# A first weight chunk of 768 columns instead of 512 in a two-layer transformer kernel

## The chip, the cores and the metric

The kernel runs on one NeuronCore of a Trainium2 chip. The metric is the device time of one execution in microseconds. A run here is one program that computes both layers from the inputs in HBM to the output in HBM.

## The reference, cut to what matters

The reference has two blocks over a sequence of 256 tokens of width 2048, everything in float32. Only the first block is touched:

```python
proj = x @ w_in + b_in                    # (256, 2048) @ (2048, 5376)
c_val, c_glu, c_gate, q, k, v, a_gate = split(proj, (1024, 1024, 1024, 1024, 128, 128, 1024))
h = c_val * sigmoid(c_glu)
h = causal depthwise convolution of h, 31 taps, per channel, + conv_b
y_conv = silu(layer_norm(h)) * silu(c_gate)
y_attn = sliding_window_attention(q, k, v, sinks) * silu(a_gate)
y = concat([y_conv, y_attn]) @ w_out + b_out
x1 = layer_norm(2 ** 0.25 * x + y)
```

The second block (sparse attention, a gated per-layer embedding, stick-breaking attention) follows from `x1` and is the same in both kernels.

## The kernel before, in words

**Numbers.** Every matmul operand is split into a high and a low part (`fp32r`), and three products are summed: high times high, high times low, low times high. For each weight tile ScalarE makes the high part (line 281) and VectorE the low part (line 282). For the activations the same is done on lines 404 and 405.

**Chunks and granules.** The weight matrices are read in one long list of column chunks, in the order of the dictionaries `CHUNKS_1`, `CHUNKS_O1` and so on. A chunk runs over 16 row tiles (`kt`) of 128 rows. It is cut into granules, each of which is one DMA, one cast (line 281) and one subtraction (line 282). `_group` says how many row tiles go into a granule: 1 for the first chunk `gv0`, 4 for a chunk of 256 columns, 2 for one of 512. So `gv0` has 16 granules of 128x512, and each chunk of 256 columns of `w_in` has 4 granules of 128x1024. `granules` loads up to 3 granules ahead of the one in use and converts up to 2 ahead, fewer at the very start. There are six buffers for raw weights and four each for the high and low parts.

**The first chunk.** `gv0` holds the first 256 columns of the gate of the convolution branch (two column tiles of 128) and the first 256 columns of its values (two more). `gemm_T` keeps the results transposed: for each row tile and each column tile, one matmul with 512 moving columns (line 359: high and low part of x side by side) and one with 256 (line 361). The activations x come in during this chunk: `load_x` fetches row tiles 0, 1, then 2 and 3 together, then pairs, all on the same queue (SP) between the weights. The next chunks are `g1`, `v1`, `g2`, `v2`, `g3`, `v3` (gates and values of the other three quarters, 256 columns each), then `kv`, the queries and gates of the attention (eight chunks) and the gate `cg` of the convolution branch (four chunks).

**PSUM.** `gemm_T` puts the first two column tiles of a chunk into one tile of two banks from the pool `acc` (two such tiles), and each further column tile into a single bank of the pool `aux` (four banks). `total` adds the two halves of a result and the bias, with a branch for a tile of two banks (lines 374 to 381) and one for a list of single banks (lines 370 and 371).

**Side work.** Work for ScalarE and VectorE that isn't a weight conversion is written as generators in lanes of `Side`. At the end of every granule, after its matmuls have been put into the program, `side.pump()` takes a step in every lane, as many `next` calls as the rate of the generator at the head says. What it puts into the program is ordered behind the subtraction of that granule (`issue_after(pace.ins)`).

```python
    def _step(self, q):
        done = 0
        while q and done < q[0][1]:
            try:
                next(q[0][0]); done += 1
            except StopIteration:
                q.popleft()
```

The lane `conv` holds eight generators `conv(ct)`, one for each 128 channels, with 31 taps each (lines 537 and 539) and a rate of 3. `glu(c)` adds two of them as soon as quarter `c` of h is there. After the `cg` chunks `conv_norm()` is added to the same lane with a rate of 1. It has seven steps: (1) sum over the channels, lines 728, 714, 715; (2) the mean, a matmul with a matrix of ones on line 720, copied on 722; (3) subtract the mean, line 735, and square, line 736; (4) sum the squares, line 738, 714, 715; (5) the variance, line 720 again; (6) `rsqrt` (lines 444 to 449), the scaling (line 746), and SiLU (line 750), the product with the gate (line 753) and the split into parts (lines 404 and 405) for channel tiles 0 to 3; (7) the same for channel tiles 4 to 7. What (6) and (7) write is `cact`, row tiles 0 to 7 of the output projection.

**The output projection.** `w_out` is used in two rounds: chunks `a0` to `a3` over row tiles 8 to 15 (the attention's half, four granules each, so 16 granules), and then chunks `c0` to `c3` over row tiles 0 to 7, which need `cact`. Between them stands `side.drain()`, which takes all the steps that are left in any lane, without a pump:

```python
    side.drain("heads")
    for c in range(NB):
        ps = gemm("w_out", f"a{c}", y1)
        ...
    side.drain()
    ln = Norm(0, z, t["ln_g"], t["ln_b"], 0)
    for c, (s, n) in enumerate(SPANS):
        ps = gemm("w_out", f"c{c}", y1)
```

The functions that the change touches:

Of the kernel before, what the change touches and what calls it, by code (L numbers as in the profile page):

```python
# [23 lines left out]
KT = D // P  # L24
# [18 lines left out]
def _c(start, n):  # L43
    return ((start, n),)
# [3 lines left out]
CV, CG, CT, QQ, KK, VV, AG = 0, 1024, 2048, 3072, 4096, 4224, 4352  # L48
# [7 lines left out]
def _twos(name, start):  # L56
# [2 lines left out]


CHUNKS_1 = {
    "gv0": ((CG, 256), (CV, 256)),
    **{f"{n}{c}": _c(o + 256 * c, 256) for c in range(1, 4) for n, o in (("g", CG), ("v", CV))},
    "kv": _c(KK, 256),
    **{f"q0{h}": _pairs(QQ, i) for i, h in enumerate("xy")},
    **{f"ag0{h}": _pairs(AG, i) for i, h in enumerate("xy")},
# [5 lines left out]
CHUNKS_1 = {key: (ranges, ALL) for key, ranges in CHUNKS_1.items()}  # L72
# [52 lines left out]
def _cols(ranges):  # L125
    return sum(n for _, n in ranges)


def _group(ranges, kts):

    if ranges == CHUNKS_1["gv0"][0]:
        return 1
    return min(len(kts), 4 if _cols(ranges) <= 256 else 2)


def _column_tiles(chunks):

    out, at = {}, 0
    for key, (ranges, _) in chunks.items():
        out[key] = at  # L140
        at += _cols(ranges) // P
    return out
# [42 lines left out]
def tile_net(ctx: ExitStack, tc: tile.TileContext, t: dict, out: bass.AP):  # L185
# [17 lines left out]
    def uid(s):  # L203
        count[0] += 1
        return f"{s}_{count[0]}"
# [5 lines left out]
    def short(shape=(P, 384), dt=F32):  # L211

        return half.tile(list(shape), dt, tag="h", name=uid("h"))

    def bank(name, n=512):
        return aux.tile([P, n], F32, tag="aux", name=uid(name))
# [17 lines left out]
    def keep(ap, base, cm, step, op, fill):  # L234
# [13 lines left out]
        for stream, key in _plan()  # L248
        for kts in (STREAMS[stream][key],)
        for g in range(0, len(kts[1]), _group(*kts))  # L250
    ]
    at = [0]
# [42 lines left out]
    def granules(stream, key, events):  # L295

        ranges, kts = STREAMS[stream][key]
        n = _cols(ranges)
        kpg = _group(ranges, kts)
        for g in range(0, len(kts), kpg):  # L300
            if events and g in events:
                events[g]()
            here = at[0]
            assert plan[here] == (stream, key, g)
            for p in plan[here:here + 1 + min(here, AHEAD)]:
                if p not in held:
                    held[p] = fetch(p)
            for p in plan[here:here + 1 + min(here, LOAD)]:
                if p not in held and p not in loaded:
                    loaded[p] = load(*p)  # L310
            hi, lo, pace = held.pop((stream, key, g))
            at[0] += 1
            for j in range(kpg):
                ws = slice(j * n, (j + 1) * n)
                yield kts[g + j], g + j == 0, g + j == len(kts) - 1, hi[:, ws], lo[:, ws]
            with tc.issue_after(pace.ins):
                side.pump()

    def gemm(stream, key, act, events=None, final=False):

        n = _cols(STREAMS[stream][key][0])
        if final:
            ps = [bank("acc") for _ in range(2)]
        else:
            both = acc.tile([P, 2, 512], F32, tag="acc", name=uid("acc"))
            ps = [both[:, tt, :] for tt in range(2)]

        def product(tt, kt, first, last, wh, wl):
            ah, al = act(kt, slice(tt * P, (tt + 1) * P))
            o = ps[tt][:, :n]  # L330
            nc.tensor.matmul(o, ah, wh, start=first, stop=False)  # L331
            nc.tensor.matmul(o, ah, wl, start=False, stop=False)  # L332
            nc.tensor.matmul(o, al, wh, start=False, stop=last)  # L333

        ends = STREAMS[stream][key][1][-_group(*STREAMS[stream][key]):]
        late = []
        for step in granules(stream, key, events):
            late.append(step)
            if step[0] in ends and not step[2]:
                continue  # L340
            for tt in range(2):
                for one in late:
                    product(tt, *one)
            late = []
        return [p[:, :n] for p in ps]

    def gemm_T(stream, key, act, events=None):

        nf = _cols(STREAMS[stream][key][0]) // P
        two = acc.tile([P, 2, 2, S], F32, tag="acc", name=uid("acc"))
        ps = [two[:, f] for f in range(2)]
        ps += [bank("acc").rearrange("p (h s) -> p h s", h=2) for _ in range(2, nf)]
        for kt, first, last, wh, wl in granules(stream, key, events):
            pair, ah = act.both(kt), act(kt, slice(0, S))[0]
            for f in range(nf):
                nc.tensor.matmul(ps[f], wh[:, f * P:(f + 1) * P], pair, start=first, stop=False)  # L359
            for f in range(nf):  # L360
                nc.tensor.matmul(ps[f][:, 0, :], wl[:, f * P:(f + 1) * P], ah, start=False, stop=last)  # L361
        return [two, ps[2:]][:nf // 2]

    def total(out_, ps, bias=None, scale=1.0):

        t = short((P, 2, S))
        out_ = t if out_ is None else out_
        if isinstance(ps, list):
            for f, p in enumerate(ps):
                nc.scalar.activation(t[:, f, :], p[:, 1, :], AF.Identity, bias=bias1[:, bias + f:bias + f + 1])  # L370
                nc.vector.tensor_tensor(out_[:, f, :], p[:, 0, :], t[:, f, :], ALU.add)
            return out_
        if bias is None:
            nc.scalar.activation(t, ps[:, :, 1, :], AF.Copy, scale=scale)  # L374
        else:
            for f in range(2):
                nc.scalar.activation(t[:, f, :], ps[:, f, 1, :], AF.Identity, bias=bias1[:, bias + f:bias + f + 1])  # L377
        if scale == 1.0:
            nc.vector.tensor_tensor(out_, ps[:, :, 0, :], t, ALU.add)  # L379
        else:  # L380
            nc.vector.scalar_tensor_tensor(out_, ps[:, :, 0, :], scale, t, ALU.mult, ALU.add)
        return out_
# [117 lines left out]
    xact = Act()  # L500

    def load_x(kt, n):
        raw = short((P, n, S))
        nc.sync.dma_start(raw, t["xT"][:, kt:kt + n, :])
        xact.put(kt, n, raw)
# [5 lines left out]
    tiles1 = _column_tiles(CHUNKS_1)  # L511
# [20 lines left out]
    def conv(ct):  # L532
        h, o = hT[ct // 4][:, ct % 4, :], cacc[ct // 4][:, ct % 4, :]
        for d in range(TAPS):
            w = convw[:, ct, TAPS - 1 - d:TAPS - d]
            if d == 0:
                nc.vector.tensor_scalar(o, h, w, convp[:, 0, ct:ct + 1], ALU.mult, ALU.add)
            else:
                nc.vector.scalar_tensor_tensor(o[:, d:], h[:, :S - d], w, o[:, d:], ALU.mult, ALU.add)  # L539
            yield  # L540

    def glu(c):
        if c == 0:
            loads = {0: (0, 1), 1: (1, 1), 2: (2, 2), **{kt - 1: (kt, 2) for kt in range(4, KT, 2)}}
            events = {kt: (lambda x=x: load_x(*x)) for kt, x in loads.items()}
            events[14] = load_params
            pg, pv = gemm_T("w_in", "gv0", xact, events)
            bg = tiles1["gv0"]
            bv = bg + 2
        else:  # L550
            pg, = gemm_T("w_in", f"g{c}", xact)
            bg, bv = tiles1[f"g{c}"], tiles1[f"v{c}"]
        sg = total(None, pg, bg)
        nc.scalar.activation(sg, sg, AF.Sigmoid)
        if c:
            pv, = gemm_T("w_in", f"v{c}", xact)
        v = total(None, pv, bv)
        nc.vector.tensor_tensor(hT[c // 2][:, 2 * c % 4:2 * c % 4 + 2, :], v, sg, ALU.mult)
        for f in range(2):
            side.add(conv(2 * c + f), CONV_RATE[f], "conv")  # L560

    QUERIES = (slice(0, 128), slice(128, 384))

# [204 lines left out]
    def residuals():  # L768
        for c in range(NB):
            residual(c)  # L770
            for _ in range(4):
                yield


    class Ple:
# [10 lines left out]
        def act(self, kt, s):  # L786
            return self.hi[:, kt, s], self.lo[:, kt, s]
# [6 lines left out]

    ple = {}
    z = {}
    glu(0)
    side.add(residuals(), 1, "residual")
    glu(1)
    nc.vector.tensor_scalar(nsink, sink, -1.0, None, ALU.mult)  # L800
    glu(2)
    glu(3)
    projected("kv", kvT)
# [22 lines left out]
    for c in range(NB):  # L826
        ps = gemm("w_out", f"a{c}", y1)
# [4 lines left out]
    for c, (s, n) in enumerate(SPANS):  # L832
        ps = gemm("w_out", f"c{c}", y1)
# [136 lines left out]
    xact = Act()  # L970
# [7 lines left out]
    for c, heads in ((0, 6), (1, 6), (2, 4)):  # L978
        ps = gemm("w_in_a_2", f"i{c}", xact)
# [109 lines left out]
    xact = block_end(0, yact, "w_out_a_2", (2, 3), False)  # L1089
# [72 lines left out]
    for c in range(4):  # L1162
# [5 lines left out]
        ps = gemm("w_kv_b_2", f"v{c}", xact)  # L1168
# [76 lines left out]
```

## Time and profile before

| | us |
|---|---|
| median of 3 runs | 1433.05 (1433.01 to 1433.28) |
| the profiled execution, its own time | 1433.75 |
| span of its trace | 1432.0 |
| TensorE matmul busy | 1422.5 (99%) |
| VectorE busy | 1031.0 (72%) |
| ScalarE busy | 799.9 (56%) |

Times in the trace are us from the start of its span. PE is TensorE's matmuls, PEld its weight loads, DVE VectorE, ACT ScalarE, SP the queue that issues nearly all DMAs. In a row of a timeline the first number is the start, the second the length of the (merged) piece, `x4` the number of instructions in it, and what stands in brackets is how long the engine had been idle and what ended that.

### The profile page before, as it was taken

To read this page: it belongs to the slowest core of one execution; us is meant where nothing else is said; L and a number is where in the kernel's file an instruction comes from. 1 tells how busy PE (TensorE), PEld (TensorE's weight loads), DVE (VectorE), ACT (ScalarE), POOL (GpSimd) and SP (SyncE) were. 2 spreads that over 40 slices of the span, in tenths; PEclk is the share of its full clock that TensorE was granted. 3 is DMA by queue.
4 is the path that set the end of the run, shared out by engine and by line. 5 is a ranking of instruction groups with operands and counts; after the bars stand their busy time and mean duration, and the time that the engine had idled before them with its cause. 6 is when DMAs were issued, how large, how long until landed. Compare 5 with 4: busy or idle time off the path is not lost.

```text
span 1432.0 us, 20420 instructions
## 1 busy us (share of the span) xinstructions
PE 1422.5 (99%) x7650; PEld 1219.4 (85%) x7650; DVE 1031.0 (72%) x1587; ACT 799.9 (56%) x1192; POOL 23.4 (2%) x51
## 2 busy tenths in 40 slices
PE   9999999999999999999999999999999999999998
PEld 7888888888998888888887888888888888888887
DVE  6999998998679868876758665655655556575854
ACT  6545877465445556655545454655656656554442
POOL 0000000000000000000000000100100001000000
PEclk9999999999999999999999999999999999999999
DMA  9765454566364555655764556455555555576462
GB/s 322 258 201 185 158 169 156 191 192 209 103 220 145 189 170 183 199 169 169 263 199 148 184 177 197 163 177 183 170 177 177 179 175 168 183 263 230 124 224 79
DMA packets 79651, 265.96 MB, mean 186 GB/s; under 512 B 9392, under 2 KB 9776, under 8 KB 79552
## 3 DMA queue, kind: packets, MB, share of 16 engines
q1 hardware_dynamic: 79488, 264.63, 56.2%
q8 instruction: 60, 0.98, 0.3%
q14 instruction: 39, 0.32, 0.1%
q0 software_dynamic: 64, 0.03, 0.0%
HBM read 262.53 MB, written 2.10 MB: 185 GB/s over the span
## 4 chain that ended last, share of the span: by engine, by line
PE 96%; DVE 2%; DMA 1%; ACT 0%; issue 0%; SPq 0%; ACTq 0%
PE acc L359 32%; PE acc L361 16%; PE acc L331 14%; PE acc L333 14%; PE acc L332 14%; PE pt L411 1%; PE pT L613 1%; DVE wlo L282 0%; PE z L1141 0%; PE z L1121 0%; PE o L648 0%; PE o L659 0%; DMA h<-in_xT 0%; PE s L581 0%; DMA h<-in_ln_g 0%; PE o L638 0%
## 5 line engine op out<-in xcount | busy, mean ns | idle before, releaser
L282 DVE TENSOR_TENSOR wlo<-raw,whi 128x1024 fp32r<-128x1024 f32 (+3 forms) x475 | 563.9, 1191 | 324.2 <-ACT whi L281 323.8
L281 ACT CAST whi<-raw 128x1024 fp32r<-128x1024 f32 (+3 forms) x475 | 487.0, 1027 | 500.5 <-PE acc L333 224.7
L359 PE MATMUL acc<-u,whi 128*128 128x512 f32 x2016 | 634.5, 397 | 1.7 <-DVE u L405 1.5
L361 PEld LDWEIGHTS acc<-u,wlo 128*128 128x128 f32 x2016 | 376.2, 188 | 88.4 <-DVE wlo L282 0.8
L361 PE MATMUL acc<-u,wlo 128*128 128x256 f32 x2016 | 394.1, 278 | 0.3 <-DVE wlo L282 0.3
L331 PE MATMUL acc<-whi,u 128*128 128x512 f32 (+2 forms) x860 | 332.3, 386 | 0.0
L332 PE MATMUL acc<-wlo,u 128*128 128x512 f32 (+2 forms) x860 | 330.1, 384 | 0.0
L333 PE MATMUL acc<-whi,u 128*128 128x512 f32 (+2 forms) x860 | 329.9, 384 | 0.0
L359 PEld LDWEIGHTS acc<-u,whi 128*128 128x128 f32 x2016 | 308.9, 189 | 6.8 <-issue 2.2
L333 PEld LDWEIGHTS acc<-whi,u 128*128 128x128 f32 x860 | 161.5, 188 | 30.8 <-DVE u L405 0.4
L331 PEld LDWEIGHTS acc<-whi,u 128*128 128x128 f32 x860 | 161.5, 188 | 29.9 <-issue 0.7
L332 PEld LDWEIGHTS acc<-wlo,u 128*128 128x128 f32 x860 | 161.6, 188 | 28.9
L539 DVE SCALAR_TENSOR_TENSOR u<-u,convw,u 128x255 f32<-128x255 f32 (+21 forms) x240 | 107.7, 465 | 2.8
L379 DVE TENSOR_TENSOR h<-acc,h 128x512 f32<-128x512 f32 x50 | 34.2, 684 | 0.4 <-ACT h L377 0.4
L594 ACT ACTIVATE u<-u,negm 128x128 f32<-128x128 f32 x64 | 28.5, 448 | 5.2 <-DVE negm L585 4.7
L1111 POOL TENSOR_SCALAR_AFFINE_SELECT h<-h 128x256 f32<-128x256 f32 x32 | 18.1, 566 | 745.1 <-DVE h L1133 715.4
L495 DVE TENSOR_TENSOR u<-u,h 128x1024 f32<-128x1024 f32 x24 | 28.7, 1219 | 1.3 <-DMA h<-in_ln_b 0.9
L404 ACT CAST u<-h 128x512 fp32r<-128x512 f32 (+1 forms) x33 | 18.4, 557 | 19.7 <-DVE h L683 17.0
L405 DVE TENSOR_TENSOR u<-h,u 128x512 fp32r<-128x512 f32 (+1 forms) x33 | 19.9, 608 | 9.1 <-ACT u L404 9.0
L281 ACT CAST u<-raw 128x1024 fp32r<-128x1024 f32 (+1 forms) x17 | 17.3, 1016 | 15.6 <-DMA raw<-in_w_ple 7.9
L374 ACT ACTIVATE h<-acc 128x512 f32<-128x512 f32 x42 | 24.9, 592 | 0.0
L482 ACT ACTIVATE h<-pt,normp 128x256 f32<-128x256 f32 x48 | 22.4, 618 | 2.8 <-PE pt L411 2.8
(207 smaller groups left out, 940.3 us busy)
## 6 DMA issues: line engine op xcount, KB each, us to landing
raw<-in_w_in_a SPq DMA_DIRECT2D x80, 512.0 KB, 3.4
raw<-in_w_in SPq DMA_DIRECT2D x76, 512.0 KB, 3.7
raw<-in_w_gate SPq DMA_DIRECT2D x64, 512.0 KB, 4.0
raw<-in_w_kv_b SPq DMA_DIRECT2D x64, 512.0 KB, 3.2
raw<-in_w_q_b SPq DMA_DIRECT2D x64, 512.0 KB, 3.3
raw<-in_w_out SPq DMA_DIRECT2D x32, 512.0 KB, 3.6
raw<-in_w_out_a SPq DMA_DIRECT2D x32, 512.0 KB, 4.2
raw<-in_w_out_b SPq DMA_DIRECT2D x32, 512.0 KB, 4.5
```

The lines of the kernel that those rows point to most:

```text
L281: nc.scalar.copy(hi, raw)
L282: return hi, lo, nc.vector.tensor_tensor(lo, raw, hi.bitcast(F32), ALU.subtract)
L331: nc.tensor.matmul(o, ah, wh, start=first, stop=False)
L332: nc.tensor.matmul(o, ah, wl, start=False, stop=False)
L333: nc.tensor.matmul(o, al, wh, start=False, stop=last)
L359: nc.tensor.matmul(ps[f], wh[:, f * P:(f + 1) * P], pair, start=first, stop=False)
L361: nc.tensor.matmul(ps[f][:, 0, :], wl[:, f * P:(f + 1) * P], ah, start=False, stop=last)
L374: nc.scalar.activation(t, ps[:, :, 1, :], AF.Copy, scale=scale)
L379: nc.vector.tensor_tensor(out_, ps[:, :, 0, :], t, ALU.add)
L495: nc.vector.tensor_tensor(self.z[c], self.z[c], r.unsqueeze(1).broadcast_to([P, 2, 512]), op)
L539: nc.vector.scalar_tensor_tensor(o[:, d:], h[:, :S - d], w, o[:, d:], ALU.mult, ALU.add)
L594: nc.scalar.activation(sc[j][:, i, cs], sc[j][:, i, cs], AF.Exp, bias=negm[j][:, i, tt:tt + 1], scale=-1.0, accum_out=den[j][:, i, tt:tt + 1],
```

## The change

The first chunk, now `gvg`, has six column tiles: gate and values of the first quarter and the gate of the second. The chunk `g1` is gone; its columns are the last third of `gvg`. `gvg` keeps one row tile per granule, so it has 16 granules of 128x768. Its first two column tiles stand in a two-bank tile of `acc`, the other four in the four single banks of `aux`. The gate of the second quarter is taken through the sigmoid at the end of the first chunk and kept until `v1` is done. `glu(1)` then runs `v1` alone.

```diff
-    "gv0": ((CG, 256), (CV, 256)),
-    **{f"{n}{c}": _c(o + 256 * c, 256) for c in range(1, 4) for n, o in (("g", CG), ("v", CV))},
+    "gvg": ((CG, 256), (CV, 256), (CG + 256, 256)),
+    **{f"{n}{c}": _c(o + 256 * c, 256) for c in range(1, 4) for n, o in (("g", CG), ("v", CV)) if (n, c) != ("g", 1)},
...
-    if ranges == CHUNKS_1["gv0"][0]:
+    if ranges == CHUNKS_1["gvg"][0]:
         return 1
...
-        return [two, ps[2:]][:nf // 2]
+        return [two, ps[2:4], ps[4:]][:nf // 2]
...
-    def glu(c):
-        if c == 0:
-            loads = {0: (0, 1), 1: (1, 1), 2: (2, 2), **{kt - 1: (kt, 2) for kt in range(4, KT, 2)}}
-            events = {kt: (lambda x=x: load_x(*x)) for kt, x in loads.items()}
-            events[14] = load_params
-            pg, pv = gemm_T("w_in", "gv0", xact, events)
-            bg = tiles1["gv0"]
-            bv = bg + 2
-        else:
-            pg, = gemm_T("w_in", f"g{c}", xact)
-            bg, bv = tiles1[f"g{c}"], tiles1[f"v{c}"]
-        sg = total(None, pg, bg)
+    def sigmoid(ps, bias):
+        sg = total(None, ps, bias)
         nc.scalar.activation(sg, sg, AF.Sigmoid)
-        if c:
-            pv, = gemm_T("w_in", f"v{c}", xact)
-        v = total(None, pv, bv)
+        return sg
+
+    def gated(c, v, sg):
         nc.vector.tensor_tensor(hT[c // 2][:, 2 * c % 4:2 * c % 4 + 2, :], v, sg, ALU.mult)
         for f in range(2):
             side.add(conv(2 * c + f), CONV_RATE[f], "conv")
+
+    def first_glu():
+
+        loads = {0: (0, 1), 1: (1, 1), 2: (2, 2), **{kt - 1: (kt, 2) for kt in range(4, KT, 2)}}
+        events = {kt: (lambda x=x: load_x(*x)) for kt, x in loads.items()}
+        events[14] = load_params
+        pg, pv, pg1 = gemm_T("w_in", "gvg", xact, events)
+        b = tiles1["gvg"]
+        sg = sigmoid(pg, b)
+        v = total(None, pv, b + 2)
+        sg1 = sigmoid(pg1, b + 4)
+        gated(0, v, sg)
+        return sg1
+
+    def glu(c, sg=None):
+        if sg is None:
+            pg, = gemm_T("w_in", f"g{c}", xact)
+            sg = sigmoid(pg, tiles1[f"g{c}"])
+        pv, = gemm_T("w_in", f"v{c}", xact)
+        gated(c, total(None, pv, tiles1[f"v{c}"]), sg)
...
-    glu(0)
+    gate1 = first_glu()
     side.add(residuals(), 1, "residual")
-    glu(1)
+    glu(1, gate1)
```

## Rows read from the trace of the kernel before

**Rows 1.** The page: busy time and share of the span, instructions.

```profile
PE   1422.5 (99%) x7650; PEld 1219.4 (85%) x7650; DVE 1031.0 (72%) x1587; ACT 799.9 (56%) x1192; POOL 23.4 (2%) x51
```

**Rows 2.** TensorE's timeline from the start to the chunk `v1`.

```profile
1.16 3.36 PE L228 MATMUL idle<-ones_mean 128*128 128x128 f32 x14 [1.16 <-DVE halfpi L925]
4.59 1.62 PE L359 MATMUL acc<-u,whi 128*128 128x512 f32 x4
6.81 1.19 PE L359 MATMUL acc<-u,whi 128*128 128x512 f32 x4
...
9.93 1.19 PE L359 MATMUL acc<-u,whi 128*128 128x512 f32 x4 [1.46 <-DVE u L405]
...
11.42 1.09 PE L359 MATMUL acc<-u,whi 128*128 128x512 f32 x4
...
28.26 1.09 PE L359 MATMUL acc<-u,whi 128*128 128x512 f32 x4
...
30.38 0.62 PE L359 MATMUL acc<-u,whi 128*128 128x512 f32 x2
...
35.25 0.63 PE L359 MATMUL acc<-u,whi 128*128 128x512 f32 x2
...
40.82 0.63 PE L359 MATMUL acc<-u,whi 128*128 128x512 f32 x2
```

**Rows 3.** All engines' timeline, 3 to 9 us: issue and conversion of row tiles 2, 3.

```profile
3.13 0.43 SPq L504 DMA_DIRECT2D h<-in_xT  x1
...
8.53 0.62 ACT L404 CAST u<-h 128x512 fp32r<-128x512 f32 x1 [0.72 <-DMA h<-in_xT]
...
9.18 0.69 DVE L405 TENSOR_TENSOR u<-h,u 128x512 fp32r<-128x512 f32 x1 [0.65 <-ACT u L404]
```

**Rows 4.** Stretches: length; busy us (x) of PE, PEld, DVE, ACT, POOL; PEclk, DMA share, GB/s.

```profile
5.00:5.50 0.50, 0.50 (x2) 0.40 (x2) 0.26 (x1) 0.27 (x1) 0.00 (x0) 1.00 0.54 193
...
8.40:9.90 1.50, 0.06 (x1) 0.00 (x0) 0.85 (x3) 1.24 (x2) 0.00 (x0) 1.00 1.06 406
...
5.00:10.00 5.00, 3.40 (x17) 2.56 (x16) 2.90 (x6) 2.97 (x6) 0.00 (x0) 1.00 0.88 307
...
260.00:275.00 15.00, 15.00 (x71) 12.50 (x70) 14.64 (x25) 6.55 (x8) 0.21 (x1) 1.00 0.59 189
```

**Rows 5.** VectorE's timeline, last taps and `conv_norm` steps 1 to 6.

```profile
272.80 0.45 DVE L539 SCALAR_TENSOR_TENSOR u<-u,convw,u 128x227 f32<-128x227 f32 x1
...
275.49 0.45 DVE L539 SCALAR_TENSOR_TENSOR u<-u,convw,u 128x226 f32<-128x226 f32 x1
275.98 1.23 DVE L728 TENSOR_TENSOR u<-u,u 128x1024 f32<-128x1024 f32 x1
...
278.97 0.42 DVE L715 TENSOR_TENSOR u<-u 128x256 f32<-128x256 f32 x1
...
299.93 1.22 DVE L282 TENSOR_TENSOR wlo<-raw,whi 128x1024 fp32r<-128x1024 f32 x1
301.06 2.35 DVE L746 TENSOR_TENSOR u<-u,h 128x1024 f32<-128x1024 f32 x2
...
304.67 0.69 DVE L753 TENSOR_TENSOR u<-u,u 128x512 f32<-128x512 f32 x1
```

**Rows 6.** TensorE's timeline: start of `a0`, mean, variance.

```profile
261.71 0.40 PE L331 MATMUL acc<-whi,u 128*128 128x512 f32 x1
...
286.21 0.60 PE L720 MATMUL cm<-u,ones_mean 128*128 128x256 f32 x2
...
296.53 0.70 PE L720 MATMUL cm<-u,ones_mean 128*128 128x256 f32 x2
```

**Rows 7.** ScalarE's timeline from the variance to the first part of `cact`.

```profile
297.27 0.38 ACT L722 COPY h<-cm 128x256 f32<-128x256 f32 x1 [1.14 <-PE cm L720]
...
303.53 2.08 ACT L750 ACTIVATE u<-u,convp 128x256 f32<-128x256 f32 x4
305.52 0.61 ACT L404 CAST u<-u 128x512 fp32r<-128x512 f32 x1
```

**Rows 8.** All engines' timeline where `c0` begins.

```profile
306.41 0.39 PE L331 MATMUL acc<-whi,u 128*128 128x512 f32 x1
...
307.00 0.19 PEld L333 LDWEIGHTS acc<-whi,u 128*128 128x128 f32 x1 [0.40 <-DVE u L405]
```

**Rows 9.** TensorE's timeline: 12 float32 passes of 128 columns in mid-run.

```profile
230.81 1.48 PE L613 MATMUL pT<-ident,u 128*128 128x128 f32 x12
```

**Rows 10.** Timelines of ScalarE and VectorE after `gv0`: values out of PSUM, `g1`'s third granule.

```profile
31.31 0.84 ACT L370 ACTIVATE h<-acc,bias 128x256 f32<-128x256 f32 x2
...
32.82 0.75 DVE L371 TENSOR_TENSOR h<-acc,h 128x256 f32<-128x256 f32 x2
33.48 1.22 DVE L282 TENSOR_TENSOR wlo<-raw,whi 128x1024 fp32r<-128x1024 f32 x1
```

## What is predicted

> **What bounds the kernel now.** The page first: TensorE's matmuls are busy 99% of the span [rows 1], so nothing but time in which TensorE stands, or runs slower, can move the end. I then looked for the places where it stands or nearly stands near the edit and near whatever the edit shifts.
>
> At the start it waits for x: row tile 2 begins at 9.93 after 1.46 us of idle, held by the low part of x on line 405 [rows 2]. That is the end of a chain: the DMA of row tiles 2, 3 is issued at 3.13, lands at 8.53, is cast, and is subtracted from 9.18 on [rows 3]. From 9.93 on the matmuls are dense: a row tile of `gv0` takes (28.26 - 11.42) / 12 = 1.40 us, one of `g1` (40.82 - 30.38) / 15 = 0.70 us [rows 2].
>
> The other place is 300 us on, where `c0` begins. It needs `cact`, the last thing that `conv_norm` writes. Its first matmul starts at 306.41, and a weight load 0.6 us later had waited 0.40 us for the low part on line 405 [rows 8]. So `conv_norm` ends just in time, with no slack at all. That is the row that decides this forecast: anything that makes `conv_norm` later is paid by TensorE in full.
>
> **The start: matmuls gained, bytes added.** Row tiles 0 and 1 run while x for row tile 2 is still coming. In the new chunk each has two more column tiles, 0.70 us each by `g1`'s step: 2 x 0.70 = 1.4 us of matmuls are taken out of later time. The rest is moved, not saved: a row tile of `gvg` costs 1.40 + 0.70 = 2.10 us.
>
> Against it stands that weight granules grow from 256 to 384 KB. Three of them (0 to 2) are ahead of the DMA of row tiles 2, 3 on the queue: 393,216 bytes more. Two more (3 and 4) are issued right behind it and share the engines: 655,360 bytes in all. Bounds: 393,216 bytes at 406 GB/s are 0.97 us, 655,360 at 193 GB/s are 3.40 us; at the 307 GB/s of the stretch from 5 to 10 us 655,360 bytes take 2.1 us [rows 4]. I take 2.1, since those transfers are in flight together. Row tile 2 then starts at 9.93 + 2.1, and `v1` at 40.82 + 2.1 - 1.4. **Term: +0.7 us (-0.4 to +2.0).**
>
> After that conversion keeps up: per 2.10 us of matmuls there are a cast and a subtraction of 768 columns, and those of 1024 columns take at most 1.22 us [rows 10].
>
> **The end of the first chunk.** Another pair of banks is emptied at once: 0.84 us on ScalarE, 0.75 on VectorE, by the values' rows [rows 10]. It is a pair that was emptied later anyway. What could suffer is the third granule of the next chunk: before, its low part was done at 34.70 and used at 35.25 [rows 2, 10], a margin of 0.55. If both pieces fell in front of it, it would be 0.84 + 0.75 - 0.55 = 1.0 us late. The four banks of `aux` and the second `acc` tile are not needed by `v1`'s matmuls, which go to the other `acc` tile. I take 0, the new chunk giving the transfers of `v1` more time; if that cover is gone it is 1.0. **Term: 0 (0 to +1.0).**
>
> **What goes with `g1`: four pumps.** This is the part of the edit that isn't written in it. Side work advances one pump per granule. `g1` had four granules, in which the first two generators of `conv` took 12 taps. In the new kernel the taps begin with `v1`. Counting pumps from the first possible tap: before 24 (`g1` to `v3`) + 36 (`kv`, queries, attention gates) + 16 (`cg`) + 16 (`a0` to `a3`) = 92; after 88. Needed: 8 x 31 = 248 taps at 3 each are 83 pumps, and `conv_norm` needs 7 more: 90. Before, 2 were to spare. After, 2 are missing: steps 1 to 5 fall on the last five granules of `a2` and `a3`, and steps 6 and 7 are left to `side.drain()`.
>
> The trace agrees with this count. The last taps (widths 227 and 226) run at 272.80 and 275.49 and step 1 at 275.98 [rows 5]; the matmul of the mean (step 2, the ninth pump of the sixteen by the count) starts at 286.21, which is (286.21 - 261.71) / 2.72 = 9 granules of 2.72 us after `a0`'s first matmul [rows 6], although its input was ready at 279.39 [rows 5]. So it is the place in the program that times it, not VectorE.
>
> After: the mean stands behind granule 13, at 286.21 + 4 x 2.72 = 297.1 (times without the start's shift). `a3` ends at 297.1 + 0.45 for the mean's own passes + 3 x 2.72 = 305.7. The variance came 296.53 - 286.21 = 10.32 us after the mean [rows 6], which would be 307.4; with less conversion between it can be ready by the end of `a3` and no sooner be issued: 305.7. I take the middle, 306.6. From the variance to `c0`: 4.53 us to the scaling, of which 1.13 are a weight conversion in between, then 2.35 of scaling, 0.69 of product on VectorE, 0.61 of cast [rows 5 to 7]; the SiLU of the first two channel tiles, which begins at 303.53 behind the first scaling [rows 7], hides under the second. That is 7.05 us without and 8.2 with that conversion; I take 7.6. `c0` starts at 306.6 + 7.6 = 314.2 instead of 306.41: 7.8 us. Bounds: 305.7 + 7.05 = 312.75 gives 6.3; 307.4 and the whole 306.41 - 296.53 = 9.88 of before gives 10.9. TensorE has nothing else: everything behind it in its queue (`c0` to `c3`, then the embedding) is in order behind `cact`. **Term: +7.8 us (+6.3 to +10.9).**
>
> The steps that follow don't add: in the drain ScalarE has 2 x 0.52 + 0.61 = 1.65 us for each pair of row tiles [rows 7], TensorE uses one in 2.72.
>
> **The clock.** In such a gap TensorE stands for some 7 us in one piece, and no row shows what it does after that; the longest idle in the run is the 1.46 us above, with a granted clock of 1.00 in every stretch that I read. The nearest row is the start, after idle: 14 passes of 128 columns take 3.36 us, 0.24 each, where 12 such passes at 230.81 take 1.48, 0.12 each; and the first four matmuls of 512 columns take 1.62 instead of 1.19 [rows 2, 9]. [...] Bounds for the gap: 0 and 2.1. I take 2.1, since a gap of 7 us is nearer to the start than to 1.46 us. **Term: +2.1 us.**
>
> [...]
>
> **Sum.** 0.7 + 0 + 7.8 + 2.1 = 10.6 us. On the profiled execution (1433.75; span 1432.0 and 1.75 around it) that is 1444.35, span 1442.6. The median of the runs is 0.70 below that execution, so 1433.05 + 10.6 = **1443.6**.
>
> **Rivals.**
>
> 1. *Not slower: `conv_norm` isn't late.* VectorE is busy 14.64 of the 15 us up to 275 [rows 4], so the taps might be timed by VectorE's queue and not by pumps; then a start that comes four pumps later is caught up in its pauses. It decides if steps 1 to 5 move up by 8 us or more. For it: that busy share. Against it: the mean stood ready for 6.8 us before its place came. What is left is the start's term: 1433.8. Chance 0.13.
> 2. *The gap without a clock loss*: 1433.05 + 8.5 = 1441.5. For it: granted clock 1.00 everywhere; against it: the slow first passes. Chance 0.20.
> 3. *A longer gap*, nothing compressed and the late granule of `v1` too: 1433.05 + 2.0 + 1.0 + 10.9 + 2.1 = 1449; about 1447 if only the gap is at its end. Chance 0.09.
> 4. *Faster*: the start pays its 1.4 us, x isn't late, and nothing is lost at `c0`: 1431.7 at best. Even this is within 0.2%. To be faster by more, the relief of VectorE would have to remove waits that the trace doesn't show. Chance 0.03.
>
> The forecast itself (gap with clock loss) has 0.55.
>
> **How the numbers follow.** About 0.2%, 2.9 us, is what a measurement here can tell from no change. Slower by more: 0.55 + 0.20 + 0.09 = 0.84. Within: rival 1, 0.13. Faster: 0.03. The likeliest case alone reaches from 1440 to 1447. The range takes in rival 2's lower end, 1433.05 - 0.4 + 6.3 = 1439, some of what lies between it and rival 1, and most of rival 3: 1437 to 1447.5. It leaves out rivals 1 and 4 and the far end of 3, just under 0.2.
>
> **What the changed profile would show.** Row tile 2 starting near 12 us and `v1` near 41.5; the row-tile step of the first chunk at 2.10 us. The last tap some 11 us later, near 286; the mean's matmul at about 298 and the variance's not before `a3`'s last matmul. A wait of TensorE of 6 to 8 us on line 405 or 404 at `c0`, and a granted clock below 1.00 after it. If TensorE has no such wait, the count of pumps or the claim that `cact` is just in time is wrong; if row tile 2 starts at 10 us, the bytes didn't matter; if the wait is there and the time is under 1441, the clock term was wrong.

## The result, and the profile after

The kernel after takes 1444.54 us (median of 4 runs, 1443.89 to 1445.82), the kernel before in the same rounds 1433.16 (1433.01 to 1433.32): a ratio of 1.0077 [1.0065, 1.009], 11.4 us slower. The profiled execution of after took 1444.16 with a span of 1442.4, 10.4 more than the execution shown before. The other 1.0 us is scatter: before, the profiled execution lay 0.6 us above the median, and after 0.4 below it.

First, TensorE's timeline from its first matmul to `v1`, the answer to [rows 2].

```profile
5.43 1.66 PE L359 MATMUL acc<-u,whi 128*128 128x512 f32 x6 [0.92 <-ACT whi L281]
7.64 1.55 PE L359 MATMUL acc<-u,whi 128*128 128x512 f32 x6
10.58 1.66 PE L359 MATMUL acc<-u,whi 128*128 128x512 f32 x6 [0.68 <-DVE u L405]
...
40.08 0.63 PE L359 MATMUL acc<-u,whi 128*128 128x512 f32 x2
```

The first matmul is 0.84 us later (5.43, before 4.59), behind the high part of the larger first granule. Row tile 2 is 0.65 us later (10.58, before 9.93). From there to `v1` the new order saves the predicted 1.4 us, so in this execution `v1` begins 0.74 us *earlier* (40.08, before 40.82).

Now the other place, TensorE's timeline from the mean to the first matmuls of `c0`, the answer to [rows 6, 8]. The lines 715 and 720 of before are 725 and 730 here, and 728 and 746 are 738 and 756.

```profile
296.36 0.60 PE L730 MATMUL cm<-u,ones_mean 128*128 128x256 f32 x2
...
304.75 0.39 PE L333 MATMUL acc<-whi,u 128*128 128x512 f32 x1
306.68 0.70 PE L730 MATMUL cm<-u,ones_mean 128*128 128x256 f32 x2 [1.54 <-DVE u L725]
314.07 0.79 PE L331 MATMUL acc<-whi,u 128*128 128x512 f32 x1 [6.70 <-ACT u L404]
...
315.52 0.63 PE L331 MATMUL acc<-whi,u 128*128 128x512 f32 x1
...
317.65 0.63 PE L333 MATMUL acc<-whi,u 128*128 128x512 f32 x1
...
319.19 0.40 PE L331 MATMUL acc<-whi,u 128*128 128x512 f32 x1
```

`a3` has run out of matmuls at 305.1. The variance stands behind it and waits 1.54 us for the sum of squares; then TensorE stands 6.70 us until the cast of `cact` is there. What fills those 6.70 us is on VectorE and ScalarE, the answer to [rows 5, 7]; these are VectorE's last tap, step 1 and scaling:

```profile
285.81 0.45 DVE L539 SCALAR_TENSOR_TENSOR u<-u,convw,u 128x226 f32<-128x226 f32 x1
286.28 1.23 DVE L738 TENSOR_TENSOR u<-u,u 128x1024 f32<-128x1024 f32 x1
...
310.18 2.36 DVE L756 TENSOR_TENSOR u<-u,h 128x1024 f32<-128x1024 f32 x2
```

The last tap came at 275.49 before, so the chain is 10.3 us later from its first step on. The clock of the stretches around the gap (columns as in [rows 4]):

```profile
305.00:308.00 3.00, 0.84 (x3) 0.30 (x2) 3.00 (x6) 1.60 (x3) 0.00 (x0) 1.00 0.55 183
308.00:315.00 7.00, 0.93 (x2) 0.60 (x3) 6.18 (x10) 5.58 (x11) 0.00 (x0) 0.55 0.33 114
315.00:317.00 2.00, 2.00 (x6) 1.61 (x6) 1.74 (x3) 2.00 (x6) 0.00 (x0) 0.50 0.04 8
317.00:319.00 2.00, 2.00 (x7) 1.52 (x6) 2.00 (x5) 2.00 (x4) 0.00 (x0) 0.51 0.00 0
319.00:321.00 2.00, 2.00 (x10) 1.65 (x9) 0.95 (x4) 1.07 (x2) 0.28 (x1) 1.00 0.00 0
```

The granted clock falls to 0.50 while TensorE stands, and is back at 1.00 at 319, after some 5 us of matmuls.

### The profile page after: what moved, and what is told of

Its sections match the earlier page's. It is cut to its first block, busy times and chain, and to the rows that moved or that the text cites. A ratio compares the mean times of both kernels' runs of the same rounds, so it can differ in the third digit from the quotient of the medians.

```text
span 1442.4 us, 20395 instructions
## 1 busy us (share of the span) xinstructions
PE 1424.2 (99%) x7650; PEld 1220.7 (85%) x7650; DVE 1033.9 (72%) x1584; ACT 798.9 (55%) x1188; POOL 23.4 (2%) x51
## 4 chain that ended last, share of the span: by engine, by line
PE 93%; DVE 4%; DMA 1%; ACT 1%; issue 1%; SPq 0%; ACTq 0%; DVEq 0%
PE acc L359 30%; PE acc L361 15%; PE acc L331 14%; PE acc L333 14%; PE acc L332 14%; DVE wlo L282 1%; PE pt L411 1%; DVE u L539 1%; PE pT L623 1%; PE z L1151 0%; PE z L1131 0%; PE o L658 0%; PE o L669 0%; DMA raw<-in_w_in 0%; DMA h<-in_b_out 0%
## 5 line engine op out<-in xcount | busy, mean ns | idle before, releaser
L282 DVE TENSOR_TENSOR wlo<-raw,whi 128x1024 fp32r<-128x1024 f32 (+2 forms) x471 | 563.4, 1199 | 329.3 <-ACT whi L281 328.6
L281 ACT CAST whi<-raw 128x1024 fp32r<-128x1024 f32 (+2 forms) x471 | 486.1, 1033 | 521.4 <-PE acc L333 237.8
L539 DVE SCALAR_TENSOR_TENSOR u<-u,convw,u 128x255 f32<-128x255 f32 (+20 forms) x240 | 108.3, 465 | 3.4
L885 DVE TENSOR_TENSOR h<-h,u 128x512 f32<-128x512 f32 x16 | 10.4, 690 | 17.7 <-ACT h L884 17.7
```

The source lines that it names most:

```text
L281: nc.scalar.copy(hi, raw)
L282: return hi, lo, nc.vector.tensor_tensor(lo, raw, hi.bitcast(F32), ALU.subtract)
```

## The experiments

The theory is the prediction's: with `g1` go four pumps, `conv_norm` ends too late, TensorE stands at `c0` and its clock falls. The first rival is that the larger chunk itself (bytes, banks, order of matmuls) makes the loss. The second is that VectorE, not the pumps, sets when the taps end. Every run is compared with the kernel before on the same chip.

**e2_hold: the lost pumps without the larger chunk.** The kernel before, in which the first two `conv` generators are added only behind the matmuls of `g1`.

```diff
             pg, = gemm_T("w_in", f"g{c}", xact)
+            if c == 1:
+                for f in range(2):
+                    side.add(conv(f), CONV_RATE[f], "conv")
...
+        if c == 0:
+            return
         for f in range(2):
```

> The kernel before, with all its chunks, and one edit: the first two generators of conv are put into their lane only after the matmuls of g1, so that the four pumps of g1 find nothing in it. No transfer, bank or chunk is changed. Theory (four pumps): c0 starts 8.4 us late as in the changed kernel against its own start (314.07 - 306.41 + 0.74), plus 2.3 us at half clock: 1433.1 + 10.7 = 1443.8. Rival (the larger chunk is what costs): 1433.1, no change.

Measured: 1443.28 (1442.32 to 1443.80), ratio 1.0063 [1.0049, 1.0077]. TensorE's timeline of this run at `c0`:

```profile
306.63 0.70 PE L725 MATMUL cm<-u,ones_mean 128*128 128x256 f32 x2 [1.54 <-DVE u L720]
314.03 0.80 PE L331 MATMUL acc<-whi,u 128*128 128x512 f32 x1 [6.70 <-ACT u L404]
```

The same two waits, to the hundredth, without one byte or bank of the new chunk. So the first rival falls for the main loss. By medians e2 loses 9.6 us and after 11.4; the intervals overlap, so these two don't resolve what the chunk itself adds.

**e1_rate5 and e3_rate4: pumps given back at once.** The kernel after, with a higher rate for the first generator: 5 gives back about four pumps, 4 about two.

```diff
-            side.add(conv(2 * c + f), CONV_RATE[f], "conv")
+            side.add(conv(2 * c + f), 5 if c + f == 0 else CONV_RATE[f], "conv")
```

> The changed kernel with one number different: the first generator of conv has a rate of 5 instead of 3. That makes up for the four pumps that went with g1: by the count, step 1 of conv_norm falls on the eighth granule of the attention half of the output projection again, and nothing is left to side.drain(). Theory (the loss is the four pumps, through the gap at c0): the gap of 6.7 us and the stretch at half clock are gone and only the start's effect is left, -0.7 us by the changed kernel's trace (v1 at 40.08 instead of 40.82): 1432.4, at most 1433.0. Rival (the chunk of 768 columns itself costs, by its larger transfers, its conversions or its four single banks): the time stays above 1440. If both hold in part, it lies between.

> The changed kernel with a rate of 4 instead of 3 for the first generator of conv: by the count two of the four lost pumps are made up, so that step 7 falls on the last granule before the drain. Theory: two granules of 2.72 us less of lateness, 8.4 - 5.4 = 3.0 us of gap at c0 left. If the gap is then too short for a fall of the clock, 1433.1 - 0.7 + 3.0 = 1435.4; if the clock falls all the same, 1437.7. Rival (a late conv_norm costs the same whenever anything of it is late): above 1440.

Measured: rate 5 gives 1437.42 (1437.07 to 1437.93), ratio 1.0025 [1.0016, 1.0034]; rate 4 gives 1444.39 (1443.43 to 1444.92), ratio 1.0071 [1.0059, 1.0084]. Both were expected faster than that. With rate 5 the gap at `c0` is gone (variance at 300.32, then dense matmuls), but another stands in its place. TensorE's timeline and the stretch 75 to 80 us of e1_rate5:

```profile
75.14 0.59 PE L361 MATMUL acc<-u,wlo 128*128 128x256 f32 x2 [2.01 <-DVE wlo L282]
...
300.32 0.70 PE L730 MATMUL cm<-u,ones_mean 128*128 128x256 f32 x2
```

```profile
75.00:80.00 5.00, 4.86 (x20) 4.24 (x21) 5.00 (x12) 0.90 (x1) 0.00 (x0) 0.66 0.52 163
```

VectorE is busy all 5.00 us there, and without a pause from 55 us on. Its own timeline:

```profile
68.13 1.21 DVE L282 TENSOR_TENSOR wlo<-raw,whi 128x1024 fp32r<-128x1024 f32 x1
69.26 2.74 DVE L539 SCALAR_TENSOR_TENSOR u<-u,convw,u 128x236 f32<-128x236 f32 x7
...
73.88 1.22 DVE L282 TENSOR_TENSOR wlo<-raw,whi 128x1024 fp32r<-128x1024 f32 x1
```

Nine taps and two other pieces of side work stand between the low parts of two granules, TensorE waits 2.01 us for the second of them, and a granted clock of 0.66 over 5 us is 1.7 us more. With `v1` 0.57 us later than before this makes 4.3, where that execution was 4.1 longer (1437.85 to 1433.75). So the pumps in `g1` were also worth VectorE's time under them: between 30 and 60 us VectorE was busy 28.32 us before and is 24.19 after, and those 4.1 us have to be found again later. The rows of before and after (columns as in [rows 4], VectorE is the third engine):

```profile
30.00:60.00 30.00, 30.00 (x174) 26.18 (x173) 28.32 (x46) 18.27 (x24) 0.00 (x0) 1.00 0.91 321
30.00:60.00 30.00, 30.00 (x173) 26.23 (x172) 24.19 (x37) 17.38 (x24) 0.00 (x0) 1.00 0.81 271
```

With rate 4 the mean comes two granules late instead of four, yet the gap is hardly smaller. TensorE's timeline of e3_rate4:

```profile
304.69 0.70 PE L730 MATMUL cm<-u,ones_mean 128*128 128x256 f32 x2
...
307.51 0.39 PE L333 MATMUL acc<-whi,u 128*128 128x512 f32 x1
314.27 0.80 PE L331 MATMUL acc<-whi,u 128*128 128x512 f32 x1 [6.37 <-ACT u L404]
```

From variance to `c0` it takes 9.58 us here and 7.39 in after. The reason is in what lies between: in e3 two casts for weights on ScalarE, and on VectorE two subtractions for weights and the two additions that empty `a3`'s results; in after it is one subtraction and the end of one such addition. Two more waits of 0.7 us at 78.5 and 82.7, for low parts again, make everything later. So 2 x 2.72 for two pumps, 1.24 more from mean to variance (11.56, before 10.32) and 1.42 of those waits are 8.1, less 0.3 in the chain and 0.2 at the start: 7.6, where `c0` is 7.86 us later than before.

**e8_before_blank1: is there slack for one pump?** The kernel before with one empty pump ahead of the first tap.

```diff
+        if c == 0:
+            side.add(iter([None]), 1, "conv")
         for f in range(2):
```

> The kernel before with one empty step ahead of the first generator of conv: one pump of the four is lost. By the count, two were to spare before the drain. Theory (there is no slack, since cact was just in time: each pump lost is paid): the variance comes one granule of 2.72 us later and c0 with it, some 2.5 us of gap: 1435.9, or up to 1437.6 if the clock falls after it as it did after the 2.0 us in e1. Rival (the two pumps to spare absorb it, and only what is left to the drain costs): 1433.4.

Measured: 1439.83 (1439.11 to 1440.48), ratio 1.0042 [1.003, 1.0055]. TensorE's and ScalarE's timelines at `c0`:

```profile
299.39 0.69 PE L722 MATMUL cm<-u,ones_mean 128*128 128x256 f32 x2
...
310.52 0.79 PE L331 MATMUL acc<-whi,u 128*128 128x512 f32 x1 [4.31 <-ACT u L404]
```

```profile
309.85 1.22 ACT L404 CAST u<-u 128x512 fp32r<-128x512 f32 x2 [0.89 <-DVE u L755]
```

One pump makes 4.31 us of wait, and the clock falls here too (0.50 from 308.5 to 315); that is more than the 1435.9 to 1437.6 expected. So of the "2 to spare" not one was slack. It costs more than its 2.72 us since from variance to `c0` it now takes 11.13 us: the product (line 755) stands behind the emptying of `a3`'s results and a weight conversion on VectorE. This run also answers the second rival. VectorE has no more work in it than before, and yet its last tap comes 2.47 us later (275.49 before), near the 2.72 of a granule:

```profile
277.96 0.45 DVE L539 SCALAR_TENSOR_TENSOR u<-u,convw,u 128x226 f32<-128x226 f32 x1
```

**e4_warm: the clock alone.** The kernel after with 27 float32 matmuls of 128 columns of ones behind the variance. They do no work of the reference and keep TensorE busy in the gap.

```diff
         var = channel_mean(sq[0])
         yield
+        warm = bank("warm")
+        for _ in range(27):
+            nc.tensor.matmul(warm[:, 0:P], ones_mean, ones_mean, start=True, stop=True)
```

> The changed kernel with 27 more matmuls (ones by ones, 128 columns, float32, result never read) put into TensorE's queue behind the variance, some 5.9 us of work at the pace of 0.109 us a pass. They fill most of the gap at c0 without making conv_norm any earlier. Theory (of the 10.4 us lost, some 2.3 are the half clock after the gap): the granted clock stays at 1.00, c0 starts at the same time, and the time falls by 2.3 us to 1442.2. Rival (the slow matmuls at c0 have another cause, such as cact coming in piece by piece): 1444.5 as the changed kernel, with the same slow matmuls.

Measured: 1443.08 (1442.37 to 1444.16), ratio 1.0062 [1.0048, 1.0076]. TensorE's timeline:

```profile
308.78 6.19 PE L755 MATMUL warm<-ones_mean 128*128 128x128 f32 x54
315.65 0.50 PE L331 MATMUL acc<-whi,u 128*128 128x512 f32 x1 [0.68 <-ACT u L404]
...
318.87 0.39 PE L331 MATMUL acc<-whi,u 128*128 128x512 f32 x1
```

The granted clock is 1.00 from 305 to 321 us. The first 12 matmuls of `c0` take 318.87 - 315.65 = 3.22 us, in after 319.19 - 314.07 = 5.12. So the lower clock costs 1.9 us. The medians differ by 1.5, with intervals that overlap, less than the 2.3 expected. The profiled executions agree with the 1.9: in e4 `v1` came 1.18 us later than in after (41.26), and the span is still 0.6 us shorter (1441.8).

**e5_spread, e7_before_spread, e6_spread_warm: pumps given back late, and the start.** Rate 4 for generators 5 and 6, in after (e5) and in before (e7); e6 is e5 with two more warm-up matmuls at the start (`WARM` 9 instead of 7).

```diff
-            side.add(conv(2 * c + f), CONV_RATE[f], "conv")
+            side.add(conv(2 * c + f), 4 if 2 * c + f in (5, 6) else CONV_RATE[f], "conv")
```

> The changed kernel with a rate of 4 for the sixth and seventh generator of conv (channel tiles 5 and 6) instead of a rate of 5 for the first. The count puts step 1 on the seventh granule, one earlier than in the kernel before. These generators run near 190 to 240 us, where VectorE was busy 25.17 us of 30 before, not at 50 to 75 us, where it was busy throughout. Theory (e1 failed to come back to 1433 only because its extra taps made VectorE late with a low part, a wait of 2.0 us and a stretch at half clock, and because its start was 0.6 us later): neither the gap at c0 nor that wait, 1433.5 within the start's scatter of -0.7 to +0.6: 1432.8 to 1434.1. Rival (VectorE has no room for the 12 taps anywhere, or the chunk itself costs 4 us): 1437 or more, with waits on line 282.

> The kernel before with the same rates as e5 (4 for the sixth and seventh generator): conv_norm comes five pumps earlier. It shows whether the kernel before itself loses anything at c0. Theory (just in time, a wait of 0.1 to 0.4 us in all): 1433.2 to 1433.6, no change that can be measured. Rival (earlier taps make VectorE late elsewhere): slower by 1 us or more; or faster by 1 us or more if c0 was held in a way that the waits don't show.

> The kernel of e5 with 9 instead of 7 warm-up matmuls at the start. In the changed kernel TensorE stood 0.8 to 0.9 us between the warm-up and the first granule, and in three of four profiles of kernels with this start the first row tiles then ran at 0.49 us a matmul of 512 columns, twice the usual. The two matmuls (four passes of 0.218 us) fill that gap. Theory (the start's gain of 1.4 us is eaten by slow matmuls after that gap): the first six matmuls take 1.7 us again, v1 starts near 40.1, and the time is 0.5 to 1.0 us below e5. Rival (the gap has nothing to do with it): no difference to e5.

Measured: e5 1435.52 (1433.67 to 1436.57), ratio 1.0013 [1.0004, 1.0022]; e7 1434.52 (1434.08 to 1435.03), ratio 1.0006 [0.9997, 1.0015]; e6 1435.13 (1433.82 to 1436.23), ratio 1.001 [1.0001, 1.0019]. There is no gap at `c0` in e5, and 9.1 of the 11.4 us are back (its kernel before took 1433.27). e7 shows that earlier taps bring the kernel before nothing that can be measured: `conv_norm` was just in time there. Both came out slower than expected, 0.9 us (e7) and 1.4 us (e5) above the top of their ranges. What both pay is a delay in the attention: the scaling of the last probabilities on ScalarE (line 618) is late for the transposes. The longest single wait is 0.43 us in e5 and 0.44 in e7, but there are smaller ones behind it, and the twelve passes take 2.78 and 2.79 us from the first to the last, 1.3 more than the 1.48 of before. TensorE's timeline of e5_spread, first the start and then the transposes that [rows 9] show in one piece:

```profile
5.43 2.93 PE L359 MATMUL acc<-u,whi 128*128 128x512 f32 x6 [0.92 <-ACT whi L281]
...
231.09 0.82 PE L623 MATMUL pT<-ident,u 128*128 128x128 f32 x6
232.34 1.53 PE L623 MATMUL pT<-ident,u 128*128 128x128 f32 x6 [0.43 <-ACT u L618]
```

e5 and e7 differ by the change alone, and neither has a gap at `c0`: 1.0 us by their medians, 0.90 by `v1` (41.25 and 40.35). That is the chunk's own price in this pair, seen without the gap. In e6 the first matmuls ran at full pace (1.69 us for six) and `v1` came at 40.30, but the median of e6 is only 0.4 below that of e5, within their scatter; what the warm-up is worth stays open.

**e10_even, e9_even_warm, e11_act_tap, e12_before_act_tap: other ways to give back four pumps.** In e10 twelve taps of generators 3 to 5 lose their step of their own; e9 is e10 with `WARM` 9. In e11 the first tap of each generator runs on ScalarE without a step, and four taps more lose theirs. e12 is the kernel before with the first tap on ScalarE and its step kept.

```diff
-            yield
+            if not (3 <= ct <= 5 and d in (6, 13, 20, 27)):
+                yield
```

```diff
-                nc.vector.tensor_scalar(o, h, w, convp[:, 0, ct:ct + 1], ALU.mult, ALU.add)
+                nc.scalar.activation(o, h, AF.Identity, bias=convp[:, 0, ct:ct + 1], scale=w)
...
-            yield
+            if d and not (2 <= ct <= 5 and d == 15):
+                yield
```

> The changed kernel in which conv leaves out 12 of its steps: in channel tiles 3, 4 and 5 the taps 6, 13, 20 and 27 are put into the program together with the tap behind them. So twelve pumps, six to eight granules apart, do one tap more, and conv_norm falls on the granules of the kernel before; nothing is done at a rate of 4 over ten pumps, and nothing near the transposes of the second attention half at 231 us, where e5 and e7 lost 1.2 us. Theory (four pumps are the whole loss, and VectorE can take the twelve taps if they are spread): no gap at c0, no wait on line 282 and no delay at 231 us; the start scatters as before, so 1433.3 with -0.7 to +0.6. Rival (VectorE has no room for them): waits on line 282 and 1435 or more.

> The kernel of e10 with 9 instead of 7 warm-up matmuls. Theory (the start's slow first row tiles follow from TensorE standing 0.9 us between warm-up and first granule): v1 starts near 40.2, and the time is 0.5 to 1 us below e10, 1432.5, just under the kernel before. Rival (the wait for x takes what the faster matmuls give): the same as e10.

> The changed kernel with the first tap of each channel tile (8 instructions of 0.41 us on VectorE) done by ScalarE in one instruction, without a step of its own, and tap 15 of channel tiles 2 to 5 put in with the tap behind it. That makes 12 steps fewer, four pumps, so conv_norm falls on the granules of the kernel before, and VectorE has 3.3 us less to do. It stood idle 4.1 us more than before between 30 and 60 us in the changed kernel (24.19 of 30 us busy, before 28.32), and that time has to come from somewhere. Theory (what g1's pumps were worth is VectorE's time in a stretch in which it is otherwise full to 280 us; e10 showed that it can't do 12 more taps later without holding up the attention's transposes by 2 us each): most of e10's 3.9 us comes back, 1434.0 to 1435.5. Rival (only the place of the steps in the program counts): no better than e10, 1437.7.

> The kernel before with the first tap of each channel tile done by ScalarE, its steps and pumps as they were. Theory (in the kernel before VectorE's load costs nothing as long as TensorE doesn't wait; cact is held by the places of the steps): 1433.3 to 1433.8, no change. Rival (VectorE is the limit in the kernel before too): faster by 1 to 3 us.

Measured: e10 1437.69 (1436.94 to 1439.27), ratio 1.0029 [1.0018, 1.0041]; e9 1437.96 (1437.70 to 1438.18), 1.003 [1.0018, 1.0041]; e11 1436.33 (1435.38 to 1436.72), 1.0018 [1.0009, 1.0027]; e12 1434.02 (1433.23 to 1436.44), 1.0003 [0.9994, 1.0011]. None has a gap at `c0`; e10, e9 and e11 were expected faster than they are. In e10 the transposes of the attention wait 1.48 us and take 4.40 from the first to the last, before 1.48, and ScalarE's timeline, then VectorE's, say for what:

```profile
231.54 0.63 ACT L527 ACTIVATE u<-h 128x512 f32<-128x512 f32 x1
232.17 1.28 ACT L610 ACT_TABLE_LOAD   x1
233.47 0.29 ACT L610 ACTIVATE es<-negm,sink 128x2 f32<-128x2 f32 x1
233.67 1.03 ACT L281 CAST whi<-raw 128x1024 fp32r<-128x1024 f32 x1
234.60 0.80 ACT L619 ACTIVATE u<-u,den 128x128 f32<-128x128 f32 x2
```

```profile
233.80 0.16 DVE L612 TENSOR_TENSOR den<-den,es 128x4 f32<-128x4 f32 x1 [3.38 <-ACT es L610]
```

The shifted order puts the activation of a gate (line 527) ahead of the attention's last exponential (line 610), and there ScalarE loads a table more, 1.28 us, and VectorE stands 3.38 us until that exponential is there. So here it isn't VectorE that holds up the rest. e9 has the same extra load at 232.74; after, e5 and e11 have no such load. e11 lies 2.65 us above its kernel before, e10 3.87: the difference is about the size of that load, but no run takes the load alone away. In both an earlier group of twelve transposes is stretched too, to 2.61 us, before 1.48 (from 177.01 on in e11, from 176.53 before). e12 shows that the move to ScalarE alone changes nothing that can be measured. No version beat the kernel before.

## Why the prediction was right

The terms, against the same execution's readings:

| term | predicted | read | from |
|---|---|---|---|
| start | +0.7 (-0.4 to +2.0) | -0.74, below the range | `v1` at 40.08, before 40.82 |
| end of the first chunk | 0 (0 to +1.0) | 0 | no wait of TensorE between 10.6 and 82 us |
| gap at `c0` | +7.8 (6.3 to 10.9) | +8.40 | 314.07 - 306.41 + 0.74 |
| clock | +2.1 (0 to 2.1) | +1.9 | e4_warm against after |
| not assigned | | +0.8 | rest to the span's 10.4 |

The step that mattered, the four pumps, was right. That the sum came so near, 10.6 us against 10.4 in these traces, is in part luck: the start was forecast 1.4 us too high, and the gap and the part that no term covers were together 1.4 too low.

**The pumps.** This step carried the forecast, and it is shown: e2_hold has the whole gap with nothing but the four pumps gone; e1, e5, e10 and e11 give pumps back in the changed kernel and the gap is gone. The mean was forecast at 297.1 without the start's shift and came at 296.36 + 0.74 = 297.10.

**The gap.** Its inner working was 0.6 short. The variance came 10.32 us after the mean, exactly as in before; it did not become ready sooner, as the middle value assumed. The conversion between had not become less: VectorE has three subtractions for weights there (at 297.64, 301.06 and 303.87), as before (287.49, 290.90 and 293.72). Then the chain was shorter than taken: 7.39 instead of 7.6. In sum: 297.10 + 10.32 + 7.39 = 314.81, less 306.41 is 8.40.

**"2 were to spare."** That part of the count was misleading. Two pumps were left in the count, but the chain behind the variance takes 9.9 us in before (306.41 - 296.53), whatever the count says, so `conv_norm` had no slack; e8 paid 4.31 us of wait for one pump. The prediction's other sentence, that `conv_norm` ends just in time, was the right one.

**The clock.** The granted clock fell to 0.50 in the gap of 6.70 us, and keeping TensorE busy there kept it at 1.00 (e4_warm), so rival 2 falls. No run shows the term of 2.1 us: it was the author's estimate from the slow passes at the start, 14 x 0.117 + 0.43 [rows 2, 9], whose number has nothing to do with the gap. What the runs show in its place is 1.9 us, e4_warm against after. That the two are so near owes something to luck.

**The start** is the term that was mis-sized in this execution. The extra bytes held x up by less than taken: its cast began at 9.15 instead of 8.53, 0.62 us later, not 2.1. The new wait, 0.92 us, is for the first granule's own cast, which the prediction did not name. But the saving isn't steady. In the seven profiles of kernels with the new chunk and `WARM` 7 `v1` begins between 40.08 and 41.39, on average at 40.84; in the five with the old chunk between 40.17 and 41.24, on average at 40.64. By these +0.2, by e5 against e7 +1.0: a small price, no gain, and a size that the scatter leaves open. Much of it goes with TensorE's pace at the start, which the term left out: where the first six matmuls take 1.66 us (after and e10_even) `v1` begins at 40.08 and 40.50, in the other five, where they take 2.93, at 40.59 to 41.39. So the early `v1` of the profiled execution is in part an accident of that execution (see the last section).

**Rival 1** was wrong as it stood: VectorE didn't time the last taps, the pumps did (e2, e8). But the busy share it rested on was real: where the taps were made up at once, VectorE was late with the weights, by 2.01 us in e1 and 1.42 in e3. Every way of giving four pumps back left the kernel some 2 to 4 us above the one before. Of this the traces show the waits and the stretched transposes named above and e10's table load. In e5, whose span is 1.5 us longer than before, these are 0.43 us at `v1` and 1.3 at the transposes; what makes the rest in e11 wasn't isolated.

What stays open is the rest of 0.8 us: 0.2 of it had come by 356 us, the other 0.6 behind that, where both kernels run the same code.

## What to carry to other kernels

When a stage is removed, count what rides on its steps: here four slots for side work went with it, and the chain that they fed was already just in time. Read slack from the wait at the consumer (0.40 us at `c0`), not from slots that a count leaves over. And a slot is worth the engine time under it: 4.1 us of VectorE that lie idle early were not to be had for nothing later, where it is full (e1: 5.00 of 5 us busy, and TensorE waits 2.01 us) or where another order costs ScalarE a table load (e10: 1.28 us).

## What was not expected of the hardware

A single wait of 2.01 us in an otherwise dense stretch (e1_rate5, 75 us) was followed by a granted clock of 0.50 from 75.4 to 78.8, so that it fell when TensorE was already at work again, while after a wait of 1.54 us (e4_warm, at 308.25) it stayed at 1.00, and after 1.46 us the next four matmuls took 1.19 us as at full pace [rows 2]. In e3_rate4 its mean from 307 to 314 us is 0.90 and it is 0.50 from 314 on: it fell near 312.6, some 4.7 us after TensorE had stopped. No limit can be read from these.

The first matmuls run at either of two paces with the same 0.92 us of idle ahead of them: six took 1.66 us in after and 2.93 in e5_spread. The first six of `c0` in after, at a granted 0.50, take the same 2.93 us (from 314.07 to 317.00). The slow pace ends in the second granule. TensorE's timeline of e5_spread:

```profile
8.16 1.48 PE L361 MATMUL acc<-u,wlo 128*128 128x256 f32 x6
9.44 1.86 PE L359 MATMUL acc<-u,whi 128*128 128x512 f32 x6
...
11.13 0.88 PE L361 MATMUL acc<-u,wlo 128*128 128x256 f32 x6
```

The column of the granted clock gives 1.00 for all of this. That is no reading: from 5.4 to 8.4 us it gives 1.00 for e5_spread, with 8 matmuls in that time, and 1.00 for after, with 16. So there only the pace of the matmuls tells. In the five profiles with the old chunk the first four take 1.19 to 2.08 us and the next four 1.19 to 1.21. With `WARM` 9 the first six take 1.69 (e6) and 2.22 (e9), the next six 1.65 and 1.55. In the seven with the new chunk and `WARM` 7 the first six take 1.66 twice and 2.93 five times, and behind the 2.93 the next six take 1.56 to 2.14. In these seven TensorE stands 0.77 to 0.92 us behind the warm-up. That this idle time can put off the full pace is a guess: two of the seven had it from their first matmul on all the same.
